# A hybrid SSD and attention layer: sums of the prologue by adding transfers, T1 and T2 out of PSUM, and work moved between the engines

## The chip, the cores and the metric

The kernel runs on one core of a Trainium2 chip. The metric is the device time of one execution in microseconds (us). The engines go by their names in the profile: PE (TensorE), DVE (VectorE), ACT (ScalarE), POOL (GpSimd) and SP (SyncE, which here only issues transfers). PEld is PE's weight load, which runs beside its matmuls.

## The reference

One decoder layer on x (1024 tokens by 1024 channels, float32):

```python
h = _rmsnorm(x, pre_g)
proj = einsum('bld,de->ble', h, w_in)      # z_ssm | xBC | dt | q | k | v | f | z_att | g_ssm | g_att
...                                        # A: conv, SiLU, chunked Mamba-2 scan, gated norm -> y_ssm
...                                        # B: attention with logits q.k/8 + F[t] - F[s]     -> y_att
merged = sigmoid(g_ssm) * (y_ssm @ w_branch_ssm) + sigmoid(g_att) * (y_att @ w_branch_att)
out = x + _rmsnorm(merged @ w_out, post_g)
```

What matters here is the start: h is normed, turned so that channels lie on the partitions, and multiplied by the columns of w_in. dt and f are two narrow sets of 16 columns each, the other columns are taken in units of 128.

## The kernel before, in words

**Products by seven multiplications.** Every large product is computed for a pair of 128-column units at a time (class Pair). Of the weights, a11 and a12 are the two halves (by rows) of the first unit, a21 and a22 those of the second. Of h, turned, b11, b12, b21 and b22 are blocks of 512 channels by 512 tokens (first index: half of the channels, second: half of the tokens). Instead of eight block products there are seven, called steps 1 to 7:

- weights: 1: a11, 2: a12, 5: s1 = a21 + a22, 6: s2 = s1 + a11, 7: a11 + a21, 4: a22, 3: s2 + a12 (signs are put on the other operand)
- the operand from h: 1: b11, 2: b21, 5: T1 = b12 - b11, 6: -T2 with T2 = b22 - T1, 7: T3 = T2 - b11, 4: T4 = T2 - b21, 3: -b22

Each operand is held in two parts, a rounded one made by ACT and the rest made by DVE (`split` at L345 for weights, `put` at L1211 for the blocks of h). A step is 12 matmuls: four blocks of 128 rows, three each (high by high, high by low, low by high). In the profile the operands of h are x0h/x0l (b11), x1 (b21), x2 (-b22), x3 (T1), x4 (-T2), x5 (T3) and x6 (T4); the weights' operand is `wop`; raw weights are `raw`, sums of them `sum`.

**The stream of steps.** Class Stream holds the list of all steps (L476 on). With p, q and r the first three pairs it begins (p,1) (q,1) (p,2) (q,2) (p,6) (p,5) (p,7) (p,4) (p,3) (q,6) (q,5) (q,7) (r,1) (q,4) (q,3). Code elsewhere calls `stream.halves(n)`, which issues the next n half steps. At the start of a step `ahead` (L597) prepares the weights' operand of the step that is three further on, from step 0 on (the first three are prepared in `begin`). `load_more` (L509) loads raw weights, two tiles of 256 KB at a time on SP's queue, into six buffers; it goes on when all uses (table USES) of the two oldest have been prepared. `total` (L353) adds two weight halves on DVE; for p and q all sums are made by DVE.

**Order.** Instructions without a mark are put in order on their engines when the kernel is built, by a model of the times. Those in `pin`, and all matmuls and turns, keep the order of the program on their engine. Each engine and each queue of transfers runs its instructions in that order, and waits at the first that isn't ready.

**The prologue**, from L1167. Eight tiles of x (128 tokens each) are loaded. `norm_tiles` (L1191) takes the sum of squares (ACT, or DVE for tiles 1 and 3), the root (ACT), its reciprocal (DVE) and scales the tile: DVE for tiles 0 to 3, GpSimd for 4 to 7. `turned` (L1205) turns four 128x128 blocks by PE into a PSUM tile `pt` (two buffers). First half of the tokens, L1225: for k = 0 to 7 the turned tile times the norm's gain is copied to `low[k]` (DVE for k = 0, 1; ACT for the others) and put as b11 (k < 4) or b21; from k = 4 on, each k is followed by a half step: (p,1) and (q,1) run here.

Then 12 transfers copy w_out from DRAM to DRAM on SP's queue (L1236); the copy is read near the end of the kernel.

Second half, L1240: four rounds j = 0 to 3. A round turns two tiles (k = j, j + 4); ACT copies both, with the gain, to `up` (b12) and `b22[j]`; four matmuls with 32 columns of `wdf` (dt and f) go to four groups of 32 partitions of the PSUM tile `df`, one for each of b11, b12, b21, b22; DVE makes T1 and T2 from the copies, and both are put; a half step follows ((p,2) in rounds 0 and 1, (q,2) in 2 and 3); DVE then subtracts b11 and b21 from T2 in place, which makes T3 and T4 (L1262, L1263). After the rounds T3, T4 and -b22 are put, in that order, pinned, with half steps of (p,6), (p,5), (p,7) and (p,4) between and behind. `df` is copied with its bias to `dft`; four small matmuls with `summing` (two unit matrices side by side and below one another) add its groups up and turn them (L683).

Of the kernel before, what the change touches and what calls it, by code (L numbers as in the profile page):

```python
# [86 lines left out]
def hybrid_layer(ctx: ExitStack, tc, a, out):  # L87
# [12 lines left out]
    for n in range(2):  # L100
        nc.scalar.dma_start(bdf[32 * n : 32 * n + 32, :], a["cst"][0:32, 120:121])
# [218 lines left out]
    class Pair:  # L320
# [5 lines left out]
        USES = {"a11": (1, 6, 7), "a12": (2, 6), "a21": (6, 7), "a22": (6, 4)}  # L326

        def __init__(self, keys, handlers, ops=None, adds=nc.vector):
# [4 lines left out]
            self.s1, self.sums = None, 0  # L333

        def load(self, names):
            for n in names:
# [6 lines left out]
                self.raw[n] = t  # L343

# [13 lines left out]
        def prepare(self, which):  # L358
            r = self.raw
            self.prepared.add(which)  # L360
            if which in (5, 6) and self.s1 is None:
                self.s1 = self.total(r["a21"], r["a22"])
# [98 lines left out]
    class Stream:  # L461
# [6 lines left out]
        def __init__(self, pairs, double, last):  # L468
# [6 lines left out]
            p, q, r = pairs[0:3]  # L475
            self.steps = [(p, 1), (q, 1), (p, 2), (q, 2)] + [(p, n) for n in (6, 5, 7, 4, 3)]  # L476
# [32 lines left out]
        def load_more(self):  # L509

            while self.loads:
# [5 lines left out]
                if not all(set(p.USES[n]) <= p.prepared for p, n in old):  # L517
                    return
# [8 lines left out]
        def prepare(self, p, which):  # L527
            p.prepare(which)
            self.load_more()
# [637 lines left out]
    with tc.tile_pool(name="pro", bufs=1, reuse_waits="tile", side="right") as pro, tc.tile_pool(  # L1167
# [5 lines left out]
        nc.scalar.dma_start(preg, a["cst"][:, 80:88])  # L1173
        ss = pro.tile([P, NT], F32, name="ss")
# [16 lines left out]
        def norm_tiles(hf, tiles):  # L1191
            for t, xt in enumerate(tiles, 4 * hf):
# [7 lines left out]
                if hf == 0:  # L1200
                    nc.vector.tensor_scalar(xt, xt, rstd[:, t : t + 1], None, ALU.mult)
                else:
                    nc.gpsimd.tensor_scalar(xt, xt, rstd[:, t : t + 1], None, ALU.mult)
# [15 lines left out]

        tiles = load_tiles(0)  # L1220
# [4 lines left out]
        for k in range(NK):  # L1225
            pt = turned(tiles, k)
            if k > 1:
                nc.scalar.activation(low[:, k, :], pt, AF.Copy, scale=preg[:, k : k + 1])
            else:
                nc.vector.tensor_scalar(low[:, k, :], pt, preg[:, k : k + 1], None, ALU.mult)  # L1230
            put("b11" if k < KH else "b21", k % KH, low[:, k, :])
# [3 lines left out]

        for k, h in [(k, h) for j in range(KH) for k, h in ((j, 0), (j + KH, 0), (j + KH, 1))]:  # L1236
            pin(nc.sync.dma_start(wo_dram[k, :, half(h)], a["wo"][k * P : (k + 1) * P, half(h)]))

        b22 = []
        for j in range(KH):  # L1240
            up = []
# [3 lines left out]
            for k in (j, j + KH):  # L1245
# [547 lines left out]
```

## Time and profile before

| | us |
|---|---|
| median of 3 runs (1277.46 to 1280.73) | 1277.86 |
| the profiled execution | 1273.87 |
| its span, first to last instruction | 1272.2 |
| POOL busy | 319.3 (25%) |
| mean DMA rate over the span | 184 GB/s |

The span is what the trace covers; the profiled execution's own time has 1.7 us more around it. Views used: the page (busy time of each engine), waits (who waited, for whom: total, times, longest), stretches (a table of busy time by time window), the chain of waits (the chain of work that ended last, in order of time: start, length, what), the timeline (start, length, engine, line, operation, out<-in, in brackets the idle time before it and what ended it), groups of instructions by line (count, busy time, mean ns, idle before), and the transfers of a tile. Matmuls are pipelined: records overlap, and a following matmul may start before the record of the one ahead ends.

### The profile page before, as it was taken

The page shows a single profiled execution, that of the slowest core. Times are in us where ns is not written, and L with a number is a line of the kernel's source. Part 1 is how long each engine was busy: PE and PEld are TensorE (multiplying, and loading weights), DVE is VectorE, ACT ScalarE, POOL GpSimd, SP SyncE. Part 2 cuts the span into 40 slices and gives each one's busy share as a digit, 9 for nine tenths or more (in the row PEclk, how much of TensorE's full clock was granted, in tenths as well). Part 3 has the DMA queues.
Part 4 walks back from the last instruction along what each step waited for, and adds up shares of the span by engine and source line. Part 5 has one row for each costly group of instructions (what it writes and reads, how often), then busy time and mean ns, then how long its engine had stood idle before and what let it go on. Part 6 is the DMA issues. An engine that isn't in the chain of part 4 may idle for free.

```text
span 1272.2 us, 20822 instructions
## 1 busy us (share of the span) xinstructions
PE 1246.1 (98%) x6926; PEld 982.3 (77%) x6926; DVE 1012.9 (80%) x1994; ACT 794.3 (62%) x1737; POOL 319.3 (25%) x322
## 2 busy tenths in 40 slices
PE   5999999999999999999999999999999999999997
PEld 3678888888888888888887777777777777778886
DVE  7988886988888978997767676767789767886975
ACT  7745665556665765566555666666687666844753
POOL 4000440013400241115102124223112212356062
PEclk9999999999999999999999999999999999999999
DMA  8232452545436533744447576666687657766933
GB/s 300 69 120 76 146 162 88 191 152 182 138 101 215 175 127 117 219 146 140 142 149 252 162 228 212 217 214 218 232 286 263 224 184 249 249 221 199 364 110 105
DMA packets 152236, 233.56 MB, mean 184 GB/s; under 512 B 15201, under 2 KB 60737, under 8 KB 152129
## 3 DMA queue, kind: packets, MB, share of 16 engines
q1 hardware_dynamic: 136064, 196.08, 47.7%
q10 hardware_dynamic: 10560, 18.06, 3.8%
q0 software_dynamic: 5504, 18.09, 3.7%
q8 instruction: 54, 0.88, 0.3%
q14 instruction: 54, 0.43, 0.1%
HBM read 162.99 MB, written 72.34 MB: 185 GB/s over the span
## 4 chain that ended last, share of the span: by engine, by line
PE 86%; DMA 4%; DVE 4%; ACT 4%; issue 1%; SPq 0%; POOL 0%; DVEq 0%; ACTq 0%; POOLq 0%
PE pb L128 36%; PE pc L128 21%; PE pd L128 7%; PE av L128 5%; PE pt L131 5%; PE s L128 5%; PE yps L128 2%; PE st L128 1%; ACT ex L1509 1%; DMA xt<-in_x 1%; PE tr L131 1%; PE tr_v L131 1%; DMA v<-v_dram 1%; PE df L128 1%; DVE wop L350 1%
## 5 line engine op out<-in xcount | busy, mean ns | idle before, releaser
L350 DVE TENSOR_TENSOR wop<-sum,wop 128x512 fp32r<-128x512 f32 x180 | 140.2, 780 | 53.6 <-ACT wop L349 52.6
L349 ACT ACTIVATE wop<-sum 128x512 fp32r<-128x512 f32 x180 | 112.5, 626 | 109.0 <-DVE sum L355 52.4
L1509 ACT ACTIVATE ex<-ex,nm 128x512 f32<-128x512 f32 (+1 forms) x192 | 116.2, 606 | 71.9 <-DVE nm L1505 71.6
L402 ACT ACTIVATE s<-pb 128x512 f32<-128x512 f32 x144 | 85.3, 593 | 98.2 <-PE pb L128 96.2
L128 PE MATMUL pb<-x0h,wop 128*128 128x512 f32 x384 | 131.5, 399 | 0.0
L128 PE MATMUL pb<-x6h,wop 128*128 128x512 f32 x384 | 129.5, 395 | 1.3 <-ACT s L402 1.3
L128 PE MATMUL pb<-x5h,wop 128*128 128x512 f32 x384 | 130.1, 396 | 0.7 <-ACT s L402 0.7
L350 DVE TENSOR_TENSOR wop<-raw,wop 128x512 fp32r<-128x512 f32 x144 | 105.4, 733 | 31.8 <-ACT wop L349 31.5
L128 PE MATMUL pc<-x3h,wop 128*128 128x512 f32 x384 | 129.8, 396 | 0.5 <-DVE ot L419 0.4
L128 PE MATMUL pc<-x2h,wop 128*128 128x512 f32 x384 | 130.2, 397 | 0.0
L128 PE MATMUL pb<-x4h,wop 128*128 128x512 f32 x384 | 129.1, 395 | 0.0
L1505 DVE CUSTOM_DVE_ANT_0 ex<-s,fb 128x512 f32<-128x512 f32 (+1 forms) x192 | 96.8, 552 | 20.0 <-PE s L128 14.8
L349 ACT ACTIVATE wop<-raw 128x512 fp32r<-128x512 f32 x144 | 89.7, 623 | 14.7 <-PE pd L128 6.1
L128 PE MATMUL pd<-x1h,wop 128*128 128x512 f32 x288 | 96.3, 394 | 0.0
L128 PEld LDWEIGHTS pb<-x6h,wop 128*128 128x128 f32 x384 | 72.1, 188 | 18.6 <-issue 2.0
L128 PEld LDWEIGHTS pb<-x5h,wop 128*128 128x128 f32 x384 | 72.1, 188 | 18.4 <-issue 2.0
L128 PEld LDWEIGHTS pb<-x0h,wop 128*128 128x128 f32 x384 | 72.6, 189 | 17.6 <-issue 2.9
L128 PEld LDWEIGHTS pc<-x3h,wop 128*128 128x128 f32 x384 | 72.1, 188 | 17.7 <-issue 1.5
L128 PEld LDWEIGHTS pc<-x2h,wop 128*128 128x128 f32 x384 | 72.1, 188 | 17.4 <-issue 2.4
L128 PEld LDWEIGHTS pb<-x4h,wop 128*128 128x128 f32 x384 | 72.1, 188 | 16.7 <-issue 1.9
L211 POOL TENSOR_TENSOR wd<-wd 128x256 f32<-128x256 f32 x32 | 32.4, 1011 | 205.0 <-DMA wd<-in_wo 135.0
L131 PE MATMUL pt<-ident,ex 128*128 128x128 f32 x576 | 75.1, 273 | 2.0 <-ACT ex L1509 1.4
(318 smaller groups left out, 2993.6 us busy)
## 6 DMA issues: line engine op xcount, KB each, us to landing
raw<-in_wu SPq DMA_DIRECT2D x128, 256.0 KB
csb<-cs_dram SPq DMA_DIRECT2D x32, 256.0 KB
q<-q_dram SPq DMA_DIRECT2D x32, 256.0 KB
k<-k_dram SPq DMA_DIRECT2D x16, 512.0 KB
fb<-f_dram SPq DMA_DIRECT2D x16, 512.0 KB
rb<-st_dram SPq DMA_DIRECT2D x48, 128.0 KB
wd<-in_wo SPq DMA_DIRECT2D x40, 128.0 KB
xt<-in_x SPq DMA_DIRECT2D x8, 512.0 KB
```

The source lines that it names most:

```text
L128: return tc.keep_in_program_order(nc.tensor.matmul(*args, **kw))
L131: return tc.keep_in_program_order(nc.tensor.transpose(out_, in_, idn))
L211: pin(nc.gpsimd.tensor_tensor(t[out_], t[a_], t[b_], ALU.subtract))
L349: nc.scalar.activation(op[:, 0], src, AF.Copy)
L350: nc.vector.tensor_tensor(op[:, 1], src, op[:, 0], ALU.subtract)
L402: nc.scalar.activation(s, ps, AF.Copy)
L1505: nc.vector.tensor_tensor_reduce(o, s[e][:, 0:w], fb[hp, h][:, e, 0:w], 1.0, 3.0e38, ALU.add, ALU.min, nm)
L1509: pin(nc.scalar.activation(o, o, AF.Exp, scale=-1.0, bias=nm, accum_out=hd.at(hd.sm, i, h, e)))
```

## The change

- **Adding transfers for weights.** Pairs p, q and r are marked `gathers`. `gather` loads a21 on SP into a `sum` tile and adds a22 to it by an accumulating transfer from GpSimd's queue: that is s1. For p ("fully") a second tile gets a22 and then a11 added: s2. For q and r ("partly") DVE still adds a11 to s1 to make s2. The sum for step 7 is made by adding a11 to the raw tile of a21, that for step 3 by adding a12 to s2 after step 6's operand has been made. p gathers behind the norm of the second half, q and r when step 5 of the pair ahead is prepared. Raw tiles come free after fewer uses (FEWER).
- **Adding transfers for T3 and T4.** `low` now holds the negated blocks, so T3 and T4 are sums: b11 and b21 of each round get T2 added by transfers from GpSimd's queue, but for b11 of the last round, which stays on DVE. Puts of b11 and b21 take a sign of -1.
- **T1 and T2 out of PSUM.** DVE makes both from the turned tile in PSUM (one instruction each, times the gain, with T1's other operand from SBUF); ACT copies only b22. `df` gets T1 in place of b12, in the order -b11, -b21, T1, b22; signs go in with the bias, and `summing` has one block more.
- **Moved.** The tile t = 7 of x is scaled by DVE; low[2] and low[3] are copied by DVE. The operands of steps 4 and 5 of the list, (p,6) and (p,5), are both prepared at step 2, and none at step 1. The 12 copies of w_out stand behind the puts of -b22.

The core of the diff:

```diff
-    for n in range(2):
-        nc.scalar.dma_start(bdf[32 * n : 32 * n + 32, :], a["cst"][0:32, 120:121])
+    nc.scalar.dma_start(bdf[0:32, :], a["cst"][0:32, 120:121])
...
+        FEWER = {"a11": (1, 6), "a12": (2,), "a21": (7,), "a22": (4,)}
...
                 self.raw[n] = t
+            if self.gathers and self.s1 is not None and "a21" in names:
+                self.add(self.raw["a21"], "a11")
+
+        def source(self, n):
+            return column_halves(self.keys[int(n[1]) - 1])[int(n[2]) - 1]
+
+        def add(self, t, n):
+            with tc.issue_after(self.behind) if self.behind else nullcontext():
+                nc.gpsimd.dma_start(t, self.source(n), accum_op=ALU.add)
+
+        def gather(self):
+
+            for n in range(2 if self.gathers == "fully" else 1):
+                t = wp.tile([P, KH, P], F32, tag="sum", bufs=2, name="sum")
+                nc.sync.dma_start(t, self.source("a21"))
+                self.add(t, "a22")
+                if n == 0:
+                    self.s1 = t
+                else:
+                    self.add(t, "a11")
+                    self.s2 = t
+            if "a21" in self.raw:
+                self.add(self.raw["a21"], "a11")
...
             elif which == 6:
-                self.s2 = self.total(self.s1, r["a11"])
+                if self.gathers != "fully":
+                    self.s2 = self.total(self.s1, r["a11"])
                 self.split(6, self.s2)
+                if self.gathers:
+                    self.add(self.s2, "a12")
+                    return
...
+            elif which == 7 and self.gathers:
+                self.split(7, r["a21"])
...
             p, q, r = pairs[0:3]
+            p.gathers, q.gathers, r.gathers = "fully", "partly", "partly"
...
             p.prepare(which)
+            following = self.pairs[self.pairs.index(p) + 1 :][:1]
+            if which == 5 and following and following[0].gathers:
+                following[0].gather()
             self.load_more()
...
-            if self.at + 3 < len(self.steps):
-                p, which = self.steps[self.at + 3]
+            for n in {1: (), 2: (4, 5)}.get(self.at, (self.at + 3,)):
+                if n >= len(self.steps):
+                    return
+                p, which = self.steps[n]
...
+        less = pro.tile([P, NK], F32, name="less")
+        nc.vector.tensor_scalar(less, preg, -1.0, None, ALU.mult)
...
-                if hf == 0:
+                if hf == 0 or t == 7:
                     nc.vector.tensor_scalar(xt, xt, rstd[:, t : t + 1], None, ALU.mult)
...
+        def steps_of(n, k, m):
+            j = k % KH
+            mm(df[32 * n : 32 * n + 32, :], wdf[:, k, :], m, start=(j == 0), stop=(j == KH - 1))
...
-            if k > 1:
-                nc.scalar.activation(low[:, k, :], pt, AF.Copy, scale=preg[:, k : k + 1])
+            if k >= KH:
+                nc.scalar.activation(low[:, k, :], pt, AF.Copy, scale=less[:, k : k + 1])
             else:
-                nc.vector.tensor_scalar(low[:, k, :], pt, preg[:, k : k + 1], None, ALU.mult)
-            put("b11" if k < KH else "b21", k % KH, low[:, k, :])
+                nc.vector.tensor_scalar(low[:, k, :], pt, less[:, k : k + 1], None, ALU.mult)
+            put("b11" if k < KH else "b21", k % KH, low[:, k, :], -1.0)
...
         norm_tiles(1, tiles2)
-
-        for k, h in [(k, h) for j in range(KH) for k, h in ((j, 0), (j + KH, 0), (j + KH, 1))]:
-            pin(nc.sync.dma_start(wo_dram[k, :, half(h)], a["wo"][k * P : (k + 1) * P, half(h)]))
+        stream.pairs[0].gather()
...
-            for k in (j, j + KH):
-                pt = turned(tiles2, k)
-                up.append(b22[j] if k >= KH else pro.tile([P, HALF], F32, tag="up", bufs=1, name="up"))
-                nc.scalar.activation(up[-1], pt, AF.Copy, scale=preg[:, k : k + 1])
+            pt, pt2 = turned(tiles2, j), turned(tiles2, j + KH)
             b11, b21 = low[:, j, :], low[:, j + KH, :]
-            for n, (k, m) in enumerate(((j, b11), (j, up[0]), (j + KH, b21), (j + KH, up[1]))):
-                mm(df[32 * n : 32 * n + 32, :], wdf[:, k, :], m, start=(j == 0), stop=(j == KH - 1))
             with tc.high_priority():
                 t1 = small()
-                nc.vector.tensor_tensor(t1, up[0], b11, ALU.subtract)
+                nc.vector.scalar_tensor_tensor(t1, pt, preg[:, j : j + 1], b11, ALU.mult, ALU.add)
                 put("t1", j, t1)
-                t2 = small()
-                nc.vector.tensor_tensor(t2, up[1], t1, ALU.subtract)
+            nc.scalar.activation(b22[j], pt2, AF.Copy, scale=preg[:, j + KH : j + KH + 1])
+            steps_of(0, j, b11)
+            steps_of(2, j + KH, b21)
+            steps_of(1, j, t1)
+            steps_of(3, j + KH, b22[j])
+            with tc.high_priority():
+                t2 = pro.tile([P, HALF], F32, tag="up", bufs=2, name="t2")
+                nc.vector.scalar_tensor_tensor(t2, pt2, preg[:, j + KH : j + KH + 1], t1, ALU.mult, ALU.subtract)
                 last = put("-t2", j, t2, -1.0)
             stream.halves(1)
 
-            with tc.issue_after(last[1]) if j == KH - 1 else nullcontext():
-                nc.vector.tensor_tensor(b11, t2, b11, ALU.subtract)
-                nc.vector.tensor_tensor(b21, t2, b21, ALU.subtract)
+            if j < KH - 1:
+                nc.gpsimd.dma_start(b11, t2, accum_op=ALU.add)
+            else:
+                nc.vector.tensor_tensor(b11, t2, b11, ALU.add)
+            nc.gpsimd.dma_start(b21, t2, accum_op=ALU.add)
         dft = small("dft")
-        nc.scalar.activation(dft, df, AF.Identity, bias=bdf)
+        nc.scalar.activation(dft, df, AF.Identity, bias=bdf, scale=sign)
...
         for j in range(KH):
             put("-b22", j, b22[j], -1.0, order=pin)
+        for k, h in [(k, h) for j in range(KH) for k, h in ((j, 0), (j + KH, 0), (j + KH, 1))]:
+            pin(nc.sync.dma_start(wo_dram[k, :, half(h)], a["wo"][k * P : (k + 1) * P, half(h)]))
...
+        nc.vector.tensor_copy(summing[0:32, 32:64], ident[0:32, 0:32])
```

More of the change, by code (lines that the diff above doesn't have):

```diff
@@ L360, in prepare @@
             self.prepared.add(which)
-            if which in (5, 6) and self.s1 is None:
+            if which in (5, 6) and self.s1 is None and not self.gathers:
                 self.s1 = self.total(r["a21"], r["a22"])
@@ L516, in load_more @@
                         return
-                if not all(set(p.USES[n]) <= p.prepared for p, n in old):
+                if not all(set((p.FEWER if p.gathers else p.USES)[n]) <= p.prepared for p, n in old):
                     return
```

9 lines of the change are left out of this document (7 added, 2 removed).

## The prediction

> **What bounds the kernel now.** I read the page first, for which engine fills the span; then what TensorE (PE) waited for over the whole run; then a table by stage.
>
> ```profile
> span 1272.2 us, 20822 instructions
> PE 1246.1 (98%) x6926; PEld 982.3 (77%) x6926; DVE 1012.9 (80%) x1994; ACT 794.3 (62%) x1737; POOL 319.3 (25%) x322
> ```
> ```profile
> PE pb L128 <- ACT s L402: 2.0, 2, 1.3
> ...
> PE pt L131 <- ACT low L1228: 1.4, 1, 1.4
> PE pt L131 <- POOL xt L1203: 0.6, 1, 0.6
> PE pt_df L128 <- DVE summing L1304: 0.5, 1, 0.5
> PE pb L128 <- DVE x4l L1217: 0.3, 1, 0.3
> ```
> ```profile
> 32.00:45.40 13.40, 13.40 (x67) 7.25 (x66) 12.10 (x20) 9.28 (x14) 0.00 (x0) 1.00 0.06 21
> 45.40:60.10 14.70, 12.56 (x57) 9.54 (x55) 14.48 (x28) 12.32 (x24) 0.93 (x2) 1.00 0.21 76
> 60.10:70.00 9.90, 9.90 (x46) 8.20 (x45) 8.43 (x17) 4.35 (x9) 0.52 (x1) 1.00 0.48 161
> ```
> (Columns of the last: stretch, length, busy PE, PEld, DVE, ACT, POOL, clock, DMA share, GB/s.) PE is busy 98% of the span, and its waits outside the start-up lie nearly all in the prologue, before 60 us: of those quoted only 0.7 of the 2.0 on `s` comes later (a wait of 1.3 is quoted below). From 60.1 on PE has no gap. So the change, which works on the prologue, is worth the time by which PE reaches that gapless stretch sooner, and no more; work taken off DVE after 60 us is off the path already. The clock is 1.00 in these stretches.
>
> In the prologue the chain of waits shows who holds PE (start, length, what):
>
> ```profile
> 12.01 1.16 ACT sqt L1197 x2
> ...
> 16.80 1.15 ACT low L1228 x2
> ...
> 24.11 0.52 ACT wop L349
> ...
> 27.83 0.52 ACT wop L349
> 28.34 0.58 ACT up L1248
> ...
> 28.97 1.62 PE df L128 x6
> ...
> 32.18 0.87 PE pt L131 x8
> 33.05 2.02 PE df L128 x8
> ```
> From 12.01 to 28.92 every piece is ACT, so ACT sets the first of the four rounds (turn, dt/f matmuls `df`, half a step `pd`). Then PE goes round by round.
>
> **The change, part by part.**
>
> *ACT's chain up to round 0.* Tiles 2 and 3 of the first half go from ACT to DVE (the L1228 x2 above, 1.15). The operands of steps (p,6) and (p,5), the two L349 pieces (0.52 each), are made from step 2 on, behind round 0's turned tiles. T1 comes out of PSUM on DVE, so `up` (0.58) goes. That is 1.15 + 0.52 + 0.52 + 0.58 = 2.77 off an unbroken ACT chain. What is late next: PE cannot turn the second half before GpSimd has scaled its tiles.
>
> ```profile
> 14.20 12.89 POOL L1203 TENSOR_SCALAR xt<-xt,rstd 128x1024 f32<-128x1024 f32 x4 [12.83 <-DVE rstd L1199]
> ```
> One takes 12.89 / 4 = 3.2, so three end at 14.20 + 9.7 = 23.9; with the fourth on DVE the turns could start at 24 instead of 27, sooner than ACT is free (28.92 - 2.77 = 26.15). The PE wait on POOL (0.6) goes with the rest. DVE takes two copies and a scaling and gives back sums:
>
> ```profile
> L1230 DVE TENSOR_SCALAR low<-pt,preg 128x512 f32<-128x512 f32 x2 | 1.5, 751 | 0.6 <-PE pt L131 0.6
> L355 DVE TENSOR_TENSOR sum<-sum,raw 128x512 f32<-128x512 f32 x2 | 2.1, 1047 | 0.0
> L355 DVE TENSOR_TENSOR sum<-raw 128x512 f32<-128x512 f32 x4 | 2.7, 687 | 0.6 <-DMA raw<-in_wu 0.6
> L1263 DVE TENSOR_TENSOR low<-th,low 128x512 f32<-128x512 f32 x4 | 2.7, 685 | 0.0
> ```
> Added: 1.5 for two copies, about 0.75 for tile 7 (same row's mean as the nearest price). Removed before round 0: three sums of pair p, 0.7 + 2.1, and the add of a12 at L371. So DVE is no later, and I count nothing. Bounds for this part: 0 (the scheduler puts other ACT work into the room) to 4.0 (PE bound by 24.9, the end of turning after 23.9). I take **2.8**, the sum of rows.
>
> *Rounds 1 to 3.* In round 1:
>
> ```profile
> 32.71 0.69 ACT L1248 ACTIVATE up<-pt,preg 128x512 f32<-128x512 f32 x1 [0.85 <-PE pt L131]
> 33.30 0.68 ACT L1248 ACTIVATE b<-pt,preg 128x512 f32<-128x512 f32 x1
> ...
> 34.03 1.04 PE L128 MATMUL df<-b,wdf 128*32 128x512 f32 x2
> ...
> 35.01 0.50 PE L128 MATMUL pd<-x1h,wop 128*128 128x512 f32 x1
> ```
> The turned tiles are done at 33.05 (32.18 + 0.87). The second copy waits for the first and ends at 33.98; the last `df` starts at 34.03, `pd` at 35.01. In the change T1 is made by DVE while ACT copies b22, so the copy ends 33.0 + 0.68 = 33.7: 0.33 sooner. Nothing else of the round shrinks. Bounds: 0 (T1 late on DVE) to 1.08 (`df` never waits: 0.98 after 33.05). I take 3 x 0.33 = **1.0**. T2 too reads PSUM, so DVE reads PSUM twice a round. The row for that:
>
> ```profile
> 36.69 0.69 DVE L415 TENSOR_TENSOR th<-pd,s 128x512 f32<-128x512 f32 x1 [0.49 <-PE pd L128]
> ```
> 0.69, as from SBUF (L1263 above): nothing. [...]
>
> *T3, T4 and the sums by adding transfers.* Seven of eight subtractions (0.6 to 0.7 each by the L1263 row) go to GpSimd's queue: over 4 us of DVE in the stretch 32 to 60, where DVE is busy 26.6 of 28.1; two sums of q go too, against two operand splits moved in. So -t2 is ready when (p,6) begins, and t3, t4 and -b22 follow sooner:
>
> ```profile
> 45.42 0.40 PE L128 MATMUL pb<-x4h,wop 128*128 128x512 f32 x1
> ...
> 48.17 0.50 PE L128 MATMUL pb<-x4l,wop 128*128 128x512 f32 x1 [0.30 <-DVE x4l L1217]
> ...
> 48.74 0.39 PE L128 MATMUL pc<-x3h,wop 128*128 128x512 f32 x1
> ```
> ```profile
> 53.98 0.39 PE L128 MATMUL pb<-x5h,wop 128*128 128x512 f32 x1
> ...
> 55.03 0.59 ACT L402 ACTIVATE s<-pb 128x512 f32<-128x512 f32 x1
> ...
> 55.67 0.50 PE L128 MATMUL pb<-x6h,wop 128*128 128x512 f32 x1 [1.31 <-ACT s L402]
> ```
> ```profile
> 63.14 2.72 PE pb L128 x12
> ```
> (p,6) ran from 45.42 to 48.74, 3.3, against 2.72 for a step with no wait: **0.6** back. PE stood 1.3 before (p,4): (p,7)'s last matmul had ended at 54.4 (53.98 + 0.39), the copy `s` began at 55.03, so 0.6 of it is ACT's queue. ACT reaches these operands earlier by what DVE no longer does; I take **0.5** (bounds 0 and 0.6), the rest being the copy itself. The 0.5 on `summing` goes as DVE has about 4 us less: **0.5** (bounds 0 and 0.5).
>
> *What is costed at nothing.* The 12 copies of w_out leave SP's queue at 12.0 and come back behind -b22:
>
> ```profile
> 12.00 10.54 SPq L1237 DMA_DIRECT2D wo_dram<-in_wo  x12
> ...
> 61.30 8.06 SPq L342 DMA_DIRECT2D raw<-in_wu  x4
> ```
> ```profile
> 80.41 0.63 ACT L349 ACTIVATE wop<-sum 128x512 fp32r<-128x512 f32 x1 [2.00 <-DVE sum L355]
> ```
> They hold SP 10.5 us, with the loads that now stand at 61.3 queued behind them. Were SP to reach them as late as 55, these loads would slip to 65.5, 4 us late; but the operand that needs their sum, r's, is split at 80.4, so over 10 us of cover stays. If that cover were gone, each us that SP is late would be one of PE. GpSimd's extra issues lie on an engine that is idle from 27.1 (14.20 + 12.89) and has 0.00 in 32 to 45; signs and `less` are single small DVE instructions at the start.
>
> **Sum:** 2.8 + 1.0 + 0.6 + 0.5 + 0.5 = **5.4 us**. The profiled execution took 1273.87, of it 1.7 outside the span, and would take 1268.5; the median of the runs shown is 1277.86, 4 above it, so on that scale **1272.5 us**.
>
> **The rivals.**
>
> *Back to back anyway.* PE goes on in its order; only waits that the trace calls waits go: 1.4 (low), 0.6 (POOL), 0.3 (x4l), 0.5 (`s`), 0.5 (`summing`) = 3.3, hence 1274.6. For it: the rounds show no PE idle. Against it: a modelled busy of 2.02 for `df`, whose last matmul visibly starts when the copy ends.
>
> *An adding transfer lands late, and GpSimd's queue stands in order behind it.* No row shows an adding transfer. Nearest are plain transfers of the same 256 KB from GpSimd:
>
> ```profile
> L193 POOL DMA_DIRECT2D t_s<-x x12 | 6.7, 558 | 3.0 <-POOL x L211 2.7 <-DVE ns L1422 0.3
> ```
> ```profile
> DMA to landing us min/median/max: 2.3/3.0/8.1
> ```
> With landing L: the queue is free at 23.9 and gives s1 and s2 their a22 by 25.0 (two issues of 0.56); a11 onto s2 only when that has landed, done at 25.6 + 2L. Splits of s2 and s1 by 28 + 2L, plus SP's load for q (3.0): 31 + 2L at most; two issues for q and seven for t3 and t4, 4 to 5 us: 35 + 2L; landing 35 + 3L; t3 split on ACT and DVE, 36.2 + 3L. In the forecast (p,6) begins at 45.42 - 3.8 = 41.6, (p,7) two steps of 2.72 later at 47.1, and its second half wants the last t3 at 48.4. So it costs nothing up to L = 4.1, and 3(L - 4.1) beyond. At L = 5.8 the gain is gone (about 1278); from L = 7.1 the kernel is slower by over 0.3%; at 8.1 it loses 12 and ends at 1284.5. For it: the transfer reads its target too, and 8.1 has been seen. Against: DMA is 0.06 busy from 32 to 45. [...]
>
> *It doesn't do what it says*: the order of unpinned instructions is chosen at build time, and ACT or DVE may be made to stand before an s2 that lands later than planned; that stall, one L of 3 to 6, takes back most of the 5.4: 1276.
>
> **How the numbers follow.** Forecast 0.50 (its own range 1269 to 1275); back to back 0.15; late landings with L of 4.6 to 7 0.10, about 1278; L above 7.1 0.15, about 1284; other order 0.10. Measured differences below 0.3% (3.8 us) can't be told from none. Of the forecast's 0.50 some 0.05 fall short of 3.8, and of the 3.3 case 0.05 goes beyond: faster 0.50; slower 0.17; same 0.33. The range: upward it must take in late landings to L of about 7.3, 1282; downward the upper bounds of the parts (4.0 + 3.2 + 0.6 + 0.6 + 0.5 = 8.9) give 1269.
>
> **What would show it.** Right: the chain of waits reaches the first `df` by about 26; (p,6) begins near 41.6 and (p,4) near 50.8 (55.67 - 4.9); no old L1263 on DVE but one L1262; `s` before (p,4) waits under 1 us; adding transfers land in 3 to 4 us. Wrong: ACT or DVE idle on `sum` or `raw` with a DMA as releaser, x5 operands waiting for `low`, PE waiting on x5 or x6, or new PE waits after 60 us on `raw`. The forecast fails above all if an adding transfer takes more than 5 us, or if ACT's freed room is filled ahead of round 0.

## The result, and the profile after

| | before | after |
|---|---|---|
| median of 14 runs each (lowest, highest) | 1277.13 (1274.72, 1280.73) | 1281.58 (1278.31, 1284.23) |
| ratio, 95% interval | | 1.0030, 1.0021 to 1.0039 |
| the profiled execution, its span | 1273.87, 1272.2 | 1282.82, 1281.1 |

The change makes the kernel slower by 0.3%, some 4 us. The forecast was 1272.5, a gain. First the page of the changed kernel, then its waits (who waited, for whom: total, times, longest), over the whole run:

```profile
span 1281.1 us, 20858 instructions
...
PE 1246.6 (97%) x6926; PEld 983.0 (77%) x6926; DVE 1006.7 (79%) x1985; ACT 790.2 (62%) x1731; POOL 328.5 (26%) x339
```
```profile
PE pb L127 <- ACT s L432: 3.7, 2, 3.0
PE pc L127 <- DVE th L449: 2.5, 1, 2.5
PE df L127 <- DVE th L1293: 1.5, 2, 1.1
PE pc L127 <- DVE x3l L278: 1.4, 1, 1.4
...
PE pb L127 <- DVE wop L374: 0.9, 1, 0.9
...
PE pb L127 <- DVE x4l L1260: 0.3, 1, 0.3
```
PE's work is the same (1246.6 against 1246.1), so the loss is waiting. Two waits weigh most: 3.0 on the copy `s` ahead of (p,4), which was 1.3, and 2.5 on L449 ahead of (q,5), which was not there. The waits on T1 (`th` of L1293) and on an operand split (`wop` of L374) are new too; they belong to round 0 and round 3 below. The 0.3 on x4l is still there. Now the table by stage of the kernel after (columns as in the prediction):

```profile
32.00:45.32 13.32, 12.93 (x66) 6.90 (x64) 9.91 (x15) 8.13 (x13) 6.67 (x9) 1.00 0.97 179
45.32:62.56 17.24, 13.89 (x58) 10.89 (x56) 14.02 (x27) 12.68 (x24) 2.12 (x4) 0.90 1.06 305
62.56:70.82 8.26, 5.73 (x26) 4.43 (x26) 4.37 (x9) 1.99 (x6) 1.75 (x2) 1.00 0.94 248
70.82:90.75 19.93, 19.93 (x90) 16.49 (x90) 18.29 (x42) 10.05 (x18) 0.86 (x1) 1.00 0.49 150
```
(p,6) begins at 45.32, as before (45.42): the four rounds brought nothing. (p,6) to (p,4) then take 17.24 us, at a mean clock of 0.90 where before had 1.00, and only from 70.82 on is PE without a gap. In the second row the DMA engines are full (1.06, against 0.21 in before's like stretch): that is where the 12 copies of w_out now lie.

As a mark of where PE stands at the end of the prologue I take the start of the first `pt_cs` (L127, the scan stage's first small matmuls): 85.50 before, 90.75 after, **5.25 later**. Step by step, by the starts of PE's steps in the two traces: (p,4) 1.6 late (57.29 against 55.67); (p,4) and `pt_df` at a lowered clock another 1.3, less 0.5 for the wait on `summing` that is gone: (p,3) 2.4 late; (q,5) another 2.7: 5.1 late. 5.25 is close to the 4.45 between the medians. The two profiled spans differ by 8.9; the 3.7 behind `pt_cs` is scattered (the 1.4 on x3l above, which was 0.3 before, is the largest piece), and single executions of one kernel spread over 6 us, so I leave it aside.

**Round 0: DVE took ACT's place.** The timeline of DVE ahead of round 0, kernel after (start, length):

```profile
20.58 2.52 DVE L374 TENSOR_TENSOR wop<-raw,wop 128x512 fp32r<-128x512 f32 x1
23.03 1.81 DVE L1243 TENSOR_SCALAR xt<-xt,rstd 128x1024 f32<-128x1024 f32 x1
24.77 0.67 DVE L374 TENSOR_TENSOR wop<-raw,wop 128x512 fp32r<-128x512 f32 x1
...
26.57 1.88 DVE L1260 SCALAR_TENSOR_TENSOR x1l<-low,x1h 128x512 fp32r<-128x512 f32 x3
28.38 0.73 DVE L1293 SCALAR_TENSOR_TENSOR th<-pt,preg,low 128x512 f32<-128x512 f32 x1
```
One operand split takes 2.52 where the next takes 0.67, and the scaling of tile 7 takes 1.81 for the 0.75 that the prediction gave it. PE waits 0.9 for the long split in (q,1), and T1, which was to follow the turned tiles at once, is made at 28.38, so that `df` waits another 1.1 for it. In that time GpSimd issues adding transfers and scales (its timeline):

```profile
20.32 1.06 POOL L353 DMA_DIRECT2D raw<-in_wu  x1
21.15 3.14 POOL L1245 TENSOR_SCALAR xt<-xt,rstd 128x1024 f32<-128x1024 f32 x1
```

**Round 3: the operands came back.** Rounds 1 and 2 take 4.28 each, round 3 takes 5.1 (before, each took 4.4 to 4.5). Its chain of waits:

```profile
37.68 1.03 ACT wop L373 x2
...
38.73 1.28 ACT L665
...
40.57 0.62 ACT wop L373
...
41.21 0.69 DVE wop L374
41.91 0.67 DVE th L1293
```
The splits for (p,6) and (p,5), taken out of ACT's queue ahead of round 0, stand here (the two at 37.68). A table load of 1.28, which the kernel before has at the same place (38.50), and the split for (p,7) come next, and T1 of the last round behind them.

**(p,4): the last sum lands 11 us after its issue.** The chain of waits of the kernel after goes on so, and below it is the landing of the adding transfers of T4 (line L1310):

```profile
44.98 11.12 DMA low<-t
...
56.12 0.63 ACT x6h L1256
56.75 0.49 ACT s L432
...
57.29 4.34 PE pb L127 x12
```
```profile
DMA to landing us min/median/max: 4.9/6.1/11.1
```
T2 of the last round is added to b21 by a transfer issued at 44.98. ACT waits for it at the split `x6h`, and `s`, the copy that frees PE's next step, stands behind that split. SP's timeline shows what fills the DMA engines meanwhile:

```profile
40.34 14.11 SPq L1328 DMA_DIRECT2D wo_dram<-in_wo  x12
...
60.11 0.42 SPq L1345 DMA_DIRECT2D cst<-in_cst  x1
```
**The clock falls.** The table over the 3.0 us in which PE stood, and behind it (the last three columns: clock, DMA share, GB/s):

```profile
55.70:57.29 1.59, 0.00 (x0) 0.00 (x1) 1.30 (x3) 1.17 (x3) 0.00 (x0) 1.00 1.05 389
57.29:58.50 1.21, 1.21 (x5) 1.03 (x6) 1.21 (x3) 1.21 (x3) 0.00 (x0) 1.00 1.07 376
58.50:60.00 1.50, 1.50 (x5) 1.17 (x5) 1.33 (x7) 0.30 (x1) 1.03 (x3) 0.56 1.05 359
60.00:61.40 1.40, 1.40 (x4) 1.04 (x4) 0.00 (x0) 0.00 (x0) 0.40 (x2) 0.50 1.04 304
```
**(q,5): the constants.** Their load, issued by SP behind the copies at 60.11 (53.12 before), is waited for by DVE. SP itself had waited 3.5 us for copies to land before it could issue the transfers in between.

```profile
67.02 0.20 DVE L1356 TENSOR_SCALAR cst<-cst 128x80 f32<-128x80 f32 x1 [3.14 <-DMA cst<-in_cst]
...
70.05 0.63 DVE L449 TENSOR_TENSOR th<-s,pc 128x512 f32<-128x512 f32 x1
```
What stands behind it on DVE, up to L449, is late by as much, and PE with it. The order has a share in it: here L449 stands behind the work on the constants with its reciprocal of 1.75 us (L732), while before the like of L449 ran at 63.58, ahead of the reciprocal at 66.71.

### The profile page after: what moved, and what is told of

It is laid out like the page before. It is cut to its first block, busy times and chain, and to the rows that moved or that the text cites. A ratio compares the mean times of both kernels' runs of the same rounds, so it can differ in the third digit from the quotient of the medians.

```text
span 1281.1 us, 20858 instructions
## 1 busy us (share of the span) xinstructions
PE 1246.6 (97%) x6926; PEld 983.0 (77%) x6926; DVE 1006.7 (79%) x1985; ACT 790.2 (62%) x1731; POOL 328.5 (26%) x339
## 4 chain that ended last, share of the span: by engine, by line
PE 70%; DVE 10%; DMA 9%; issue 5%; ACT 4%; POOL 1%; SPq 1%; ACTq 0%; DVEq 0%; POOLq 0%
PE pb L127 30%; PE pc L127 17%; PE pd L127 6%; PE av L127 4%; PE pt L130 4%; PE s L127 4%; DVE wop L374 2%; PE yps L127 2%; DMA raw<-in_wu 2%; DMA raw<-in_wv 1%; DVE sum L379 1%; DMA low<-t 1%; DVE xs L815 1%; ACT ex L1559 1%; PE tr_v L130 1%
## 5 line engine op out<-in xcount | busy, mean ns | idle before, releaser
L374 DVE TENSOR_TENSOR wop<-sum,wop 128x512 fp32r<-128x512 f32 x177 | 137.2, 777 | 56.7 <-ACT wop L373 55.9
L374 DVE TENSOR_TENSOR wop<-raw,wop 128x512 fp32r<-128x512 f32 x147 | 109.9, 748 | 35.4 <-ACT wop L373 34.2
L127 PE MATMUL pb<-x6h,wop 128*128 128x512 f32 x384 | 130.4, 398 | 3.0 <-ACT s L432 3.0
L127 PE MATMUL pc<-x3h,wop 128*128 128x512 f32 x384 | 129.9, 396 | 3.2 <-DVE th L449 2.5
L127 PE MATMUL pb<-x0h,wop 128*128 128x512 f32 x384 | 131.1, 398 | 0.9 <-DVE wop L374 0.9
L127 PE MATMUL pb<-x5h,wop 128*128 128x512 f32 x384 | 129.9, 395 | 0.7 <-ACT s L432 0.7
L127 PE MATMUL pc<-x2h,wop 128*128 128x512 f32 x384 | 130.2, 397 | 0.0
L127 PE MATMUL pb<-x4h,wop 128*128 128x512 f32 x384 | 129.1, 395 | 0.0
L1555 DVE CUSTOM_DVE_ANT_0 ex<-s,fb 128x512 f32<-128x512 f32 (+1 forms) x192 | 96.8, 553 | 20.6 <-PE s L127 15.3
L127 PE MATMUL pd<-x1h,wop 128*128 128x512 f32 x288 | 96.3, 394 | 0.0
L127 PEld LDWEIGHTS pb<-x6h,wop 128*128 128x128 f32 x384 | 72.5, 189 | 20.4 <-ACT s L432 3.5
L127 PEld LDWEIGHTS pc<-x3h,wop 128*128 128x128 f32 x384 | 72.1, 188 | 20.8 <-issue 4.4
L127 PEld LDWEIGHTS pb<-x0h,wop 128*128 128x128 f32 x384 | 72.2, 188 | 18.7 <-issue 2.9
L127 PEld LDWEIGHTS pb<-x5h,wop 128*128 128x128 f32 x384 | 72.1, 188 | 18.1 <-issue 2.0
L127 PEld LDWEIGHTS pc<-x2h,wop 128*128 128x128 f32 x384 | 72.1, 188 | 17.3 <-issue 2.4
L127 PEld LDWEIGHTS pb<-x4h,wop 128*128 128x128 f32 x384 | 72.1, 188 | 16.7 <-issue 1.9
L127 PE MATMUL pc<-x3l,wop 128*128 128x512 f32 x192 | 75.1, 391 | 1.4 <-DVE x3l L278 1.4
```

The costliest lines, as they stand in the source:

```text
L127: return tc.keep_in_program_order(nc.tensor.matmul(*args, **kw))
L374: nc.vector.tensor_tensor(op[:, 1], src, op[:, 0], ALU.subtract)
L1555: nc.vector.tensor_tensor_reduce(o, s[e][:, 0:w], fb[hp, h][:, e, 0:w], 1.0, 3.0e38, ALU.add, ALU.min, nm)
```

## The experiments

**Theory:** the moved copies of w_out make the change slower: they lie in the DMA engines from 40 to 54 us, so that the last T4 sum and the constants land late; without them the change is worth about nothing. **First rival:** adding transfers are slow by themselves (the prediction's late landing), and the copies only happen to lie there. **Second rival:** the new order on ACT and DVE is what costs. The edits are to the changed kernel. All times stand together here; (p,6) and `pt_cs` are starts in the profiled run, the ratio is to the kernel before.

| | median | ratio, 95% interval | (p,6) | `pt_cs` |
|---|---|---|---|---|
| after | 1281.58 | 1.0030, 1.0021 to 1.0039 | 45.32 | 90.75 |
| copies_late | 1278.04 | 1.0011, 0.9997 to 1.0024 | 45.15 | 86.39 |
| t4_dve | 1276.47 | 0.9997, 0.9986 to 1.0009 | 45.27 | 86.39 |
| tile7_pool | 1284.23 | 1.0057, 1.0045 to 1.0070 | 53.26 | 93.32 |
| copies_back | 1277.42 | 1.0001, 0.9990 to 1.0012 | 44.46 | 85.55 |
| behind_t4 | 1275.56 | 0.9995, 0.9982 to 1.0008 | 43.49 | 86.56 |
| p_dve_t4 | 1281.05 | 1.0042, 1.0027 to 1.0058 | 45.94 | 90.58 |
| p_dve_back_t4 | 1277.44 | 1.0005, 0.9990 to 1.0020 | 43.99 | 84.91 |
| plain_t4 | 1276.89, single run | | 44.71 | 85.42 |
| back_t4 | 1277.03 | 1.0004, 0.9992 to 1.0016 | 44.66 | 85.52 |
| back_behind_t4 | 1274.39 | 0.9988, 0.9977 to 0.9999 | 43.89 | 84.07 |
| no_scale_t4 | 1280.34, single run | | 45.45 | 86.61 |
| x2_early | 1277.41 | 1.0005, 0.9994 to 1.0017 | 44.29 | 87.37 |
| before_x2_early | 1280.12 | 1.0019, 1.0006 to 1.0033 | 46.85 | 89.11 |

### copies_late, copies_back: the copies elsewhere

```diff
# copies_late: from behind the puts of -b22 to behind the start of the first scan group
-        for k, h in [...]:
-            pin(nc.sync.dma_start(wo_dram[k, :, half(h)], ...))
...
             if g == 0:
+                for k, h in [...]:
+                    pin(nc.sync.dma_start(wo_dram[k, :, half(h)], ...))
# copies_back: the same lines behind `stream.pairs[0].gather()`, as in the kernel before
```


> The changed kernel with the 12 copies of w_out moved on, behind the start of the first scan group. Theory A (the copies stand in the DMA engines ahead of the last T4 add, the constants and raw loads): the last T4 add lands in 4 to 6 us instead of 11.1, the copy s before (p,4) waits under 1 us instead of 3.0, the clock stays at 1.0 there, DVE no longer waits 3.1 us for cst; 5 to 6 us faster than the changed kernel, so 1 to 2 us faster than before. Theory B (adding transfers are slow by themselves): the last T4 add still lands after 8 us or more, ACT still stands on x6h, and the time stays 3 to 5 us above before.

> The changed kernel with the 12 copies of w_out back at their old place in the program, behind p's gather. Theory A: as with the late copies in the stretch 45 to 70 (s waits under 1, cst not waited for), but the sums of p, loaded and added from 12 us on, share the DMA engines with 6 MB of copies and land later, up to 6 us: 2 to 5 us faster than the changed kernel. Theory B: no gain.

With the copies gone from the prologue (copies_late), the landing of the T4 sums (its line L1310) is

```profile
DMA to landing us min/median/max: 4.8/5.0/6.1
```
The 11.1 is gone, `s` waits 1.4, (p,4) runs at clock 1.00 and L449 waits 0.5; `pt_cs` comes 4.4 sooner. Expected were 5 to 6 us and a kernel faster than before, which it is not; SP issues the constants at 56.73 here, with no copy ahead of them, so part of their delay against before (53.12) is the order of SP's other loads. With the copies at their old place (copies_back) the constants are issued at 53.15, there is no wait on L449, and `pt_cs` is that of before within 0.1; the ratio is 1.0001. So the copies' place is what makes the change slower, and without it **the rest of the change is worth nothing**, not the 5.4 forecast (the interval allows a gain of 1.3 at most).

### t4_dve, plain_t4: the adding transfers

```diff
# t4_dve: in the last round T4 is added by DVE, as T3 is; the copies stay
             if j < KH - 1:
                 nc.gpsimd.dma_start(b11, t2, accum_op=ALU.add)
+                nc.gpsimd.dma_start(b21, t2, accum_op=ALU.add)
             else:
                 nc.vector.tensor_tensor(b11, t2, b11, ALU.add)
-            nc.gpsimd.dma_start(b21, t2, accum_op=ALU.add)
+                nc.vector.tensor_tensor(b21, t2, b21, ALU.add)
# plain_t4: t4_dve, and ", accum_op=ALU.add" taken off all three places
```


> The changed kernel with the last round's T4 made by DVE like its T3; the copies of w_out stay. Theory A: the wait before (p,4) falls from 3.0 to about 1, and if it is that wait which drops the clock to 0.5 after it, the clock stays at 1.0: 1.6 + 1.8 = 3.4 us faster than the changed kernel, about 1 us above before; the wait on the constants at (q,5), 2.5 us, stays. If the clock falls because of the transfers, it falls here too and only 1.6 comes back. Theory B says the same of the first 1.6, so this run parts only wait and clock.

> The kernel t4_dve with every adding transfer of the first three pairs and of T3 and T4 made a plain one: the additions are left out, so the sums are not what they should be; bytes, queues and waits are the same. Theory B (adding makes a transfer slow): the sums' transfers land after 3 us (median) instead of 6.2, and T3 and T4's after 2.5 to 3 instead of 4 to 6. If the landing time comes from the queue, the issue and the load, it stays at 5 to 6. The time itself should change by less than 1 us.

t4_dve leaves every copy where the change put it and takes away one transfer that is needed soon: `s` waits 0.8, the clock stays at 1.00 with the DMA engines as full as in the changed kernel, and the time is that of before:

```profile
55.00:57.00 2.00, 1.39 (x6) 1.17 (x7) 2.00 (x5) 0.56 (x2) 0.00 (x0) 1.00 1.09 315
57.00:58.50 1.50, 1.50 (x8) 1.00 (x6) 1.50 (x7) 0.87 (x2) 0.08 (x1) 1.00 1.02 336
```
So here full DMA engines alone (a share of 1.02 to 1.09) don't lower the clock, and the copies cost through that landing and what follows it. The constants also gained, which was not expected: in the order built here SP reaches their load at 56.92, and L449 waits 0.6.

plain_t4 leaves the additions out and moves the same bytes. Landing of the T3 transfers (L1307), first in t4_dve, then in plain_t4:

```profile
DMA to landing us min/median/max: 3.8/4.1/4.2
```
```profile
DMA to landing us min/median/max: 2.2/2.4/3.3
```
Adding costs 1.7 us a landing here (1.7 for T4, 5.1 and 3.4, and 2.5 for the sums of weights, 6.4 and 3.9, by the medians of their lines), and GpSimd's issue takes 0.86 to 1.2 us instead of 0.54. Yet the time without it is hardly other (1276.89, `pt_cs` 1.0 sooner). The first rival is right about the price and wrong about the place: quiet landings of 4 to 6 us are covered, the one of 11.1 is not. No run puts a plain transfer in the place of that late sum, so what a plain one would have taken beside the copies is not shown.

### tile7_pool, p_dve_t4, p_dve_back_t4: the order

```diff
# tile7_pool: tile 7 scaled by GpSimd again
-                if hf == 0 or t == 7:
+                if hf == 0:
# p_dve_t4: t4_dve, and p's sums by DVE with its operands prepared as before
-            p.gathers, q.gathers, r.gathers = "fully", "partly", "partly"
+            p.between, q.gathers, r.gathers = False, "partly", "partly"
-            for n in {1: (), 2: (4, 5)}.get(self.at, (self.at + 3,)):
+            for n in (self.at + 3,):
-        stream.pairs[0].gather()
# p_dve_back_t4: the same, and the copies at their old place
```


> The changed kernel with tile 7 of x scaled by GpSimd again. Theory C (GpSimd and DVE hold each other up, and DVE's scaling of tile 7 and the split beside it, 1.8 and 2.5 us, set round 0): DVE's split takes under 1.5 us and T1 of round 0 is made up to 2 us sooner unless GpSimd's fourth scaling (to 27 or 28) takes its place; by the end of the prologue no more than 1 us either way, as the wait before (p,4) ends with the transfer. If DVE's scaling were no burden, round 0 would come 1 us later, as before the change.

> The kernel t4_dve with the first pair's sums made by DVE again and its operands (p,6) and (p,5) prepared one step apart as before the change; q and r still use adding transfers. Theory D (the adding transfers of p make s2 land at about 37, so the two operand splits of round 0 move into rounds 2 and 3 and hold T1 there: 1.3 us of waiting on DVE): round 3 takes 4.3 instead of 5.1, the raw split isn't waited for, and (p,6) begins 1 us sooner than 45.3, but round 0 is up to 1 later as DVE has 3 sums more: net 0 to 1.5 faster than t4_dve. If DVE's sums are the dearer way, T1 of round 0 comes at 30 and the kernel is 1 to 2 us slower.

> As p_dve_t4, with the 12 copies of w_out at their old place in the program too, where p has no adding transfers to disturb. Theory A: the constants are there in time, so the wait of 0.6 to 0.8 at (q,5) and what the late loads cost after it go: 0.5 to 1 us faster than p_dve_t4, 1 to 3 us faster than the kernel before. If the copies no longer matter once T4 is DVE's, it equals p_dve_t4.

tile7_pool shows the prediction's third rival in full. Its ACT:

```profile
36.98 1.15 ACT L373 ACTIVATE wop<-sum 128x512 fp32r<-128x512 f32 x2 [4.94 <-DMA sum<-in_wu]
```
p's s2 lands behind GpSimd's later scalings; ACT and DVE stand before it with T1 of a round behind, and `df` waits 3.9; behind that wait PE's matmuls take 0.60 to 0.63 instead of 0.40 for some 3 us, as long as in the kernel after at a clock of 0.50 (0.63). At most 1 us either way had been expected. So the moved tile 7 is worth about 3 us (1.0057 less 1.0030, times 1277, is 3.4; `pt_cs` differs by 2.6): a cost avoided, which the change would otherwise have brought on itself.

With p's sums on DVE there is no such wait, (p,6) and (p,5) run without a gap in p_dve_back_t4, and `pt_cs` is 0.6 sooner than before; but `s` waits 1.4 and `summing` 1.8, and the ratio is 1.0005 (1 to 3 us faster than before had been expected). p_dve_t4 differs from it by the place of the copies alone, which reach SP at 30.55 there and lie over the rounds: 5.7 later at `pt_cs`, 1.0042, where a gain over t4_dve had been expected. A line of its chain of waits and one of its DVE timeline show how:

```profile
34.56 13.88 DMA low<-t
```
```profile
40.59 0.75 DVE L1301 SCALAR_TENSOR_TENSOR t<-pt,preg,th 128x512 f32<-128x512 f32 x1 [3.25 <-DMA low<-t]
```
T2 has two buffers (the tag `up`), and a buffer comes free only when the transfers that add it to b11 and b21 have landed. Beside the copies these take 8.9 us (the median of T3 and T4; 6.1 in p_dve_back_t4), the longest 13.9, and DVE stands 3.25 and 5.17 before T2 of the last two rounds. PE then waits 1.9 and 1.2 in (p,6), and its matmuls take 0.63 instead of 0.39 for some 3 us. This is a second case in which the copies' place decides, again by a late addition, but through the buffer it reads from.

### behind_t4, no_scale_t4: what held DVE up

```diff
# behind_t4: t4_dve, and p's adding transfers behind GpSimd's last scaling
-        norm_tiles(1, tiles2)
+        stream.pairs[0].behind = norm_tiles(1, tiles2)
# no_scale_t4: t4_dve, GpSimd's scaling of tiles 4 to 6 left out (they stay unnormed)
-                    last = nc.gpsimd.tensor_scalar(xt, xt, rstd[:, t : t + 1], None, ALU.mult)
-            return last.ins if hf else None
+                    pass
```


> The kernel t4_dve with p's adding transfers ordered behind GpSimd's scalings (the first of them now stands between the second and the third). Theory C (GpSimd holds DVE up): the split that took 2.5 us on DVE beside that transfer takes 1.5 or less and T1 of round 0 is made 1 us sooner than 28.3; up to 1 us faster than t4_dve if round 3 keeps it. If the transfer's issue is no part of it, the split stays at 2.5 and nothing changes (1276.5).

> Leaves out GpSimd's scaling of tiles 4 to 6 (so these tiles stay unnormed), with the last round's T4 added by DVE. Theory (DVE's operand split of 2.52 and its scaling of tile 7 of 1.81 are long because GpSimd works beside them): they take 0.7 to 0.8 each, T1 of round 0 starts by 26.5 instead of 28.3. Rival (they are long for another reason, the adding transfers' issues or the DMAs): they stay over 1.5 each.

The same DVE instructions, first in behind_t4, then in no_scale_t4:

```profile
20.27 1.51 DVE L374 TENSOR_TENSOR wop<-raw,wop 128x512 fp32r<-128x512 f32 x1
21.70 0.74 DVE L1243 TENSOR_SCALAR xt<-xt,rstd 128x1024 f32<-128x1024 f32 x1
...
25.69 0.75 DVE L1293 SCALAR_TENSOR_TENSOR th<-pt,preg,low 128x512 f32<-128x512 f32 x1
```
```profile
20.37 0.69 DVE L374 TENSOR_TENSOR wop<-raw,wop 128x512 fp32r<-128x512 f32 x1
20.98 0.75 DVE L1243 TENSOR_SCALAR xt<-xt,rstd 128x1024 f32<-128x1024 f32 x1
```
With GpSimd issuing and scaling 2.52 and 1.81, with its scalings alone 1.51 and 0.74, with its issues alone (no_scale_t4 issues at 19.1 and 20.6) 0.69 and 0.75. It is GpSimd's work that lengthens these two, and both kinds together the most: 2.9 us. T1 of round 0 is 2.7 sooner in behind_t4: 2.1 of it are these two instructions, 0.3 that this trace is ahead by so much before them, and the rest that one split of x1l stands behind T1. Not each split beside GpSimd is held up: the next one of L374 in behind_t4, at 22.36 beside the last scaling, took 0.68. By what GpSimd's work lengthens the one and not the other, and why the scaling of tile 7 took 1.81, no run shows.

With DVE free, round 0 does gain what the prediction said. Round 1's turns in behind_t4 (PE's timeline; 32.02 in the kernel before):

```profile
29.22 1.03 PE L130 MATMUL pt<-ident,xt 128*128 128x128 f32 x8
```
That gain does not arrive: (p,6) is 1.8 sooner than in t4_dve, `pt_cs` 0.2 later. In behind_t4 T2 of round 2 waits 2.36 for an ACT instruction that follows a table load of 1.28, ACT stands 1.55 with a copy of w_out as the releaser that the trace names, and PE waits 2.1 for `s`, after which the clock is 0.50 for some 3 us.

### back_t4, back_behind_t4: together

```diff
# back_t4: copies_back and t4_dve. back_behind_t4: copies_back and behind_t4
```


> The copies of w_out at their old place and the last round's T4 added by DVE. Theory (both edits cure the same wait, on the last T4 landing late, so they do not add): as either alone, ratio 0.998 to 1.001, s wait 0.8 to 1.1. Rival (each cures something of its own, 1.9 and 4 to 5 us): they add, pt_cs near 84, ratio 0.998 or less.

> The copies of w_out at their old place, the last round's T4 added by DVE, and p's adding transfers behind GpSimd's scalings: the three edits together. Theory (the copies made the change slower; the gain at round 0 is lost because what stands behind it, the operands of (p,4) and the summing, is no sooner): the wait on s stays near 2, pt_cs within 1 us of before's 85.5, time 1273 to 1277, ratio 0.997 to 1.000. Rival (the gain at round 0 was given back only because of the moved copies and what they delay): no PE wait on s over 1, (p,3) by 58.5, pt_cs by 83.5, ratio 0.9985 or less with the interval below 1.

Two cures of the same wait do not add: back_t4 is 1.0004. back_behind_t4 is the one kernel whose interval lies below 1, at 0.9988: 1.5 us, with `pt_cs` 1.4 sooner than before. Among so many kernels an interval that ends at 0.9999 may be chance; that `pt_cs` moved by as much speaks for a gain, in one trace. Its ACT shows where the other part of round 0's gain stays:

```profile
43.21 1.15 ACT L373 ACTIVATE wop<-sum 128x512 fp32r<-128x512 f32 x2 [1.85 <-DMA sum<-in_wu]
...
45.83 2.18 ACT L1256 ACTIVATE x5h<-low 128x512 fp32r<-128x512 f32 x4
...
52.19 2.19 ACT L1256 ACTIVATE x2h<-b 128x512 fp32r<-128x512 f32 x4
54.28 0.58 ACT L432 ACTIVATE s<-pb 128x512 f32<-128x512 f32 x1
```
The last addition to p's s2, now behind four sums of T3 and T4 in GpSimd's queue (issued at 35.37), lands at 43.2 and holds ACT till then; from there to `s` ACT runs back to back, and PE waits 1.7. That is the prediction's late landing, in a mild form.

### x2_early, before_x2_early: ACT's queue ahead of `s`

```diff
# x2_early: back_behind_t4 with this edit; before_x2_early: the kernel before with it
-            put("-b22", j, b22[j], -1.0, order=pin)
+            put("-b22", j, b22[j], -1.0)
```


> As back_behind_t4, and the puts of -b22 no longer pinned behind those of T4, so that they come into the rounds, where ACT and DVE have idle time. Theory (from 43.2 to 54.9 ACT ran back to back, and s stood behind four splits of -b22 that only (p,3) needs; the 2.7 us that round 0 gained are lost there): s follows the last matmul of (p,7) directly, the wait on it falls from 1.7 to under 1, pt_cs from 84.1 to 83.2, ratio 0.998 or less with the interval below 1. Rival (the rounds have no room either, T2 and T3 are made later by the splits that now stand ahead of them): (p,6) begins later than 43.9, pt_cs stays at 84 or later, ratio 0.9985 to 1.000.

> The kernel before with this one edit alone, the puts of -b22 unpinned. Theory (the queue of ACT ahead of s was no part of the change, it stood in before as well): the wait on s of 1.3 falls to under 0.9 and that on summing of 0.5 goes, pt_cs 85.5 to about 84.5, ratio 0.999. Rival (before's DVE was full in the rounds, 26.6 of 28.1 us from 32 to 60, so that T1 and T2 are later): the rounds take 4.7 or more instead of 4.48 each, (p,6) after 46, no gain, ratio 1.000 or over.

The order came out as meant, the splits of -b22 in the rounds and `s` right behind (p,7), and its wait is down to 0.7 in both. It did not help; the rivals were right. In x2_early x4l comes late on DVE and PE waits 2.4 in (p,6), after which its clock falls:

```profile
50.20:51.50 1.30, 1.30 (x5) 1.07 (x4) 1.30 (x4) 1.30 (x3) 0.05 (x1) 0.57 0.43 71
51.50:53.00 1.50, 1.50 (x5) 1.13 (x5) 1.50 (x4) 1.50 (x4) 0.00 (x0) 0.50 1.04 214
```
before_x2_early is slower than before by 0.19%, (p,6) 1.4 later. So it is not one instruction's place: what is moved out of one wait comes back in another, and of the up to 2.8 us gained at round 0 no kernel here kept more than 1.4 to `pt_cs`. That more would arrive if work left both DVE and ACT is argued from their full stretches, and no run shows it.

## Why the prediction was wrong

The step that failed first is "What is costed at nothing", **the 12 copies of w_out**. It asked what stands behind them on SP's queue, found only the raw loads, and gave them 10 us of cover; these loads were indeed never late for PE. It did not ask what else uses the DMA engines in the 14 us that the copies take, nor what of SP's other loads stands behind them. The runs showed in its place: the last T4 sum lands after 11.1 us (1.6 at (p,4), 1.3 more by the clock), and the constants come late (2.7 at (q,5)). This is shown by copies_late, copies_back, t4_dve and the pair p_dve_t4 and p_dve_back_t4.

The measured 1281.58 lies inside the stated range of 1269 to 1282, but by luck: its upper end had been set for late landings of T3, and the time came there by another sum and by copies that had been costed at nothing. Of the signs of being right, the first `df` came at 26.99 instead of 26, (p,6) at 45.32 instead of 41.6, (p,4) at 57.29 instead of 50.8, and `s` waited 3.0 instead of under 1.

The sum of 5.4 did not come either (copies_back: nothing). Its terms, as the kernel after has them:

- *ACT's chain, 2.8.* ACT was freed, but "DVE is no later, and I count nothing" was wrong by the 2.9 us that two DVE instructions took longer beside GpSimd, whose extra issues had been costed at nothing. Round 1's turns begin at 31.64 instead of 32.02: 0.4. The term itself was right: in behind_t4, where DVE is not held up so long, they begin 2.8 sooner.
- *Rounds 1 to 3, 1.0.* 0.2 each in rounds 1 and 2 for 0.33; in round 3, 0.7 lost behind the two operands' splits, which had been counted as gone. They had only been moved.
- *(p,6), 0.6.* Nothing: 3.31 for 3.32, since T2 of the last round is as late as it was, and x4l waits 0.3 again.
- *`s`, 0.5.* A loss of 1.7. The prediction held that DVE's freed time would bring ACT's operands sooner; ACT's own queue to `s` is as long as before, and in the kernel after it stops at x6h for a landing.
- *`summing`, 0.5.* Gone as forecast in the kernel after, but only since (p,4) is late; in copies_back it waits 1.3.
- *T1 and T2 out of PSUM.* They take 0.73 to 0.75 against 0.68 for the same operation from SBUF (x1l), 0.05 to 0.07 more, which the prediction had put at nothing; the row that it leaned on, 0.69, was of another operation.

Two slips in the working change nothing in this: the upper bound of the rounds is 3 x 0.98 = 2.9 where 3.2 was added, and 33.05 + 0.68 is 33.73, so that a round's copy ends 0.25 sooner and not 0.33.

Of the rivals, "an adding transfer lands late" was the right mechanism: medians of 3.8 (T3), 5.0 (T4) and 5.5 us (the sums of weights up to 60 us) in copies_late, which has no copies beside them, where plain ones take 2.4, 3.4 and 4.2 in plain_t4, beside the copies. That landings on one tile add was seen as well: in tile7_pool GpSimd waits 2.73 us for one addition to a sum to land before it issues the next. But it was priced at T3 ahead of (p,7), where nothing waited, and without the copies; it decided at T4 ahead of (p,4). "It doesn't do what it says" was seen in part (round 3) and whole in tile7_pool. Slower had a chance of 0.17, too little where adding transfers, DVE beside them and the copies' neighbours were three prices of which no row of before showed one.

What stays open: the 3.7 us of the profiled span behind `pt_cs`, and the rule by which the clock falls.

## What to carry to other kernels

A bulk transfer that is moved can cost by what is in flight beside it and behind it, on every queue (here a sum that took 11.1 us to land, and constants issued at 60.11 instead of 53.12): list each transfer that lands in its window with the time at which it is needed, not only the loads of its own queue. When work is taken off the engine that sets a stretch, price what is next late with the instructions as they run beside the new neighbours (here 2.52 us for a split of 0.67), and follow the gain to the end of the stretch: here ACT, DVE and GpSimd's transfers each took it in turn. An adding transfer also holds the buffer that it reads from until it has landed (3.25 us of waiting on DVE in p_dve_t4). A wait of 3.0 us on PE ahead of (p,4) cost another 1.3 us by the clock in the kernel after.

## What the runs showed of the hardware

- **Adding in a transfer** of 256 KB from GpSimd takes 1.7 us longer to land for T3 (medians 4.1 and 2.4, t4_dve and plain_t4) and 0.3 to 0.7 us longer to issue (0.86 to 1.2 against 0.54) than a plain one. Up to 80 us the packets of GpSimd's queue took 33.9% of the DMA engines' time for 4.34 MB in t4_dve, and 17.0% for 4.46 MB without the additions in plain_t4.
- **An addition beside the 12 copies** landed after up to 11.1 us (after) and 13.9 us (p_dve_t4, where the median of T3 and T4 is 8.9). Without copies beside it T4's line took 6.1 at most in copies_late, and the median of T3 and T4 is 6.1 in p_dve_back_t4.
- **TensorE's clock** fell to 0.50 for some 3 us after PE waits of 3.0 (after), 2.4 (x2_early) and 2.1 us (behind_t4), and after two waits close together, 0.4 and 1.2 (before_x2_early). After 3.9 (tile7_pool), and after 1.9 and 1.2 close together (p_dve_t4), matmuls took 0.60 to 0.63 us for some 3 us where they otherwise took 0.39 to 0.40; at 0.50 in the kernel after they took 0.63. It stayed at 1.00 after 2.5 at (q,5) in the kernel after and 1.4 (copies_late). After 2.1 in no_scale_t4 (p,4) took 3.1 us, worked out from the starts and waits, close to the 3.0 of t4_dve at 1.00 and not the 4.3 of the kernel after. So in these runs the length of a wait alone doesn't decide.
- **DVE beside GpSimd:** an operand split of 0.68 took 2.52 us (after) and 2.67 us (tile7_pool) while GpSimd scaled and issued transfers, 1.51 us beside its scalings alone (behind_t4) and 0.69 us beside its issues alone (no_scale_t4).
